# Attention value products of a two-layer hybrid mixer: issued in groups of two key tiles and two heads

## The chip, the cores and the metric

The kernel runs on one core of a Trainium2 chip. The metric is the device time of one execution in microseconds (us). It is written in a tile language with a scheduler: the Python code records operations in an order, a scheduler at build time moves them within each engine's list by priority and by its own idea of when their inputs are ready, and the chip then runs each engine's list strictly in that order, with semaphores between the engines. Engines are named as in the profile: PE (TensorE matmul), PEld (its weight load), DVE (VectorE), ACT (ScalarE), POOL (GpSimd) and SP (the queue that issues the transfers).

## The reference

Two layers of a mixer run over 640 tokens: 512 latent tokens and 128 context tokens. Each layer projects the modulated input with one matrix, runs three head groups on it, projects back and applies a layer norm. The two attention groups matter here:

```python
def gqa_attention(q, k, v):            # 8 query heads, 2 key/value heads, head width 64
    s = einsum('bqgrd,bkgd->bgrqk', qb, k) * scale
    p = softmax(s, axis=-1)
    return einsum('bgrqk,bkgd->bqgrd', p, v)

def diff_attention(q, k, v, lam):      # 4 heads, two softmax maps each, width 32 per map
    s = einsum('bqhmd,bkhmd->bhmqk', qb, k) * scale
    p = softmax(s, axis=-1)
    a = p[:, :, 0] - lam * p[:, :, 1]
    return einsum('bhqk,bkhd->bqhd', a, v)
```

Latent queries read 640 keys: 128 cached context keys and 512 latent ones. That is five key tiles of 128. Everything is float32.

## The kernel before, in words

All 640 tokens go through together. A layer has a main phase and an output phase. In the main phase a background stream (`bg_stream`) computes the input projection in 14 chunks of 256 columns. Weights and activations are split into a high part rounded to the matmul type fp32r and a low part, and each product is made of three matmuls (L347 to L349 with the weights as the stationary operand on the output of tokens by columns, L368 to L370 the other way). The weight chunks come by transfer (`wraw`, L237); ACT casts the high part `wh` (L257) and DVE subtracts to get the low part `wl` (L258).

Around this background, foreground streams are recorded step by step by a small planner (`drive`), which charges each step a planned PE time and a latency from the table `COST`. One stream scores queries against keys and finds the row maximum and sum (`s_pass`: PE L990 and L994 into the one bank pair `pS`, DVE maximum L997, ACT exponential L998). Another (`pv_stream`) makes the attention output. For two heads at a time, `pv_steps` goes over the five key tiles `kt`. `st_tile` makes the transposed score tile of keys by 512 queries in a bank `pB` (L1049 for the differential heads, L1046 and L1047 for the grouped ones; `bankB` has three buffers), and ACT takes its exponential into a tile `PT` (L1055). One step later the value product (L1111, called PV below) multiplies `PT` by the value tile and adds into the bank `pO`: head `e` writes partitions 64e to 64e+63, so the two heads use two halves of the array's columns. PV is a full float32 matmul, which the trace shows as two records, each 128 rows by 64 columns by 512. There are 16 such passes over key tiles in all (8 per layer), so 160 PV matmuls, 320 records.

`PT` tiles come from a pool of 49 general buffers. `mm` is the matmul call, `act` the activation call, `tc.high_priority()` tells the scheduler to put what is recorded inside ahead of other ready work.

Of the kernel before, what the change touches and what calls it, by code (L numbers as in the profile page):

```python
# [11 lines left out]
AF = mybir.ActivationFunctionType  # L12
# [62 lines left out]
def hybrid_kernel(ctx: ExitStack, tc: tile.TileContext, A, cst, outs):  # L75
# [10 lines left out]
    def gran(shape=(128, T), dt=F32, name="g"):  # L86
        t = gp.tile(list(shape), dt, tag="g", name=name)
        return t
# [23 lines left out]
    def bankB():  # L112
        return bank("B")
# [10 lines left out]
    mm = nc.tensor.matmul  # L124
    act = nc.scalar.activation
    dve = nc.vector
    tt = nc.vector.tensor_tensor
    stt = nc.vector.scalar_tensor_tensor

    def barrier():  # L130
        es = ExitStack()
        for e in (nc.scalar.engine, nc.vector.engine, nc.tensor.engine):
            es.enter_context(tc.issue_after(next(i for i in reversed(nc.cur_bb.bb.instructions) if i.engine == e)))
        return es
# [905 lines left out]
    def st_mm(ps, it, kt, two):  # L1040
        qs = slice(0, 512) if kt < 5 else slice(512, 640)
        q1, q2 = it["q1"][:, qs], it["q2"][:, qs]
        k1, k2 = (it[k][:, 128 * kt:128 * kt + 128] for k in ("k1", "k2"))
        n = 4 if kt < 5 else 8
        if two:
            mm(out=ps, lhsT=k1, rhs=q1, start=True, stop=False)  # L1046
            mm(out=ps, lhsT=k2[0:64 + n], rhs=q2[0:64 + n], start=False, stop=True)  # L1047
        else:
            mm(out=ps, lhsT=k1[0:96 + n], rhs=q1[0:96 + n], start=True, stop=True)  # L1049

    def st_tile(it, kt, two):
        ps = bankB()
        st_mm(ps, it, kt, two)
        pt = gran((128, 512), name="PT")
        act(pt, ps, AF.Exp)  # L1055
        return pt

    def st_ctx(items, two):
        ps = bankB()
# [46 lines left out]
    def pv_steps(items, two, value, o):  # L1106
        ready = []
        for kt in range(6):
            now = [st_tile(items[e], kt, two) for e in range(2)] if kt < 5 else []
            for e, pt in enumerate(ready):  # L1110
                mm(out=o[64 * e:64 * e + 64], lhsT=value(kt - 1, e), rhs=pt, start=kt == 1, stop=kt == 5)  # L1111
            ready = now
            yield cost["pv_e" if kt == 5 else "pv_g" if two else "pv_d"]

    def diff_pv(l, m, items, nlam, of):
        dv, cv = items[0]["v"]
        o = bankO()

        def value(kt, e):
            rows = slice(64 * e, 64 * e + 64)  # L1120
            return cv[:, rows] if kt == 0 else tok(dv)[:, kt - 1, rows]

        yield from pv_steps(items, False, value, o)
        if m == 0:
            nc.scalar.copy(of[:, 0:512], o)
        else:
            stt(out=of[:, 0:512], in0=o, scalar=nlam, in1=of[:, 0:512], op0=ALU.mult, op1=ALU.add)
# [76 lines left out]
    def gqa_pv(g, items, mf):  # L1204
        av, avc = items[0]["v"]
        o = bankO()
        cols = slice(64 * g, 64 * g + 64)
        yield from pv_steps(items, True, lambda kt, e: avc[:, cols] if kt == 0 else tok(av)[:, kt - 1, cols], o)
        nc.scalar.copy(mf[:, 0:512], o)
# [63 lines left out]
    with in_order(nc.scalar.engine, nc.vector.engine, nc.tensor.engine):  # L1273
        for j in range(4):
# [5 lines left out]
            ps = bankB()  # L1280
            for k in range(KB):
                q = k % 4
                mm(out=ps[32 * q:32 * q + 32], lhsT=sc[:, k, :], rhs=rw[k].rearrange("p s c -> p (s c)"),
                   start=(k < 4), stop=(k >= 4))
# [16 lines left out]
            for i in range(2):  # L1301
                k = 2 * j + i
# [11 lines left out]
    with barrier():  # L1314
# [4 lines left out]
        first = [gran(name="tk"), gran(name="tk")]  # L1319
# [3 lines left out]
        for l in range(L):  # L1323
            *h, defer = layer(l, h, first, defer)
            first = None
# [70 lines left out]
```

## Time and profile before

| | |
|---|---|
| median of 3 runs | 986.04 us (984.52 to 993.87) |
| the profiled execution's own time | 984.84 us |
| its span in the trace | 983.1 us |
| PE busy | 932.2 us (95%) |
| DVE busy | 599.0 us (61%) |
| ACT busy | 586.8 us (60%) |
| mean granted TensorE clock | 0.988 of full speed |

A record of a matmul on PE lasts until its result is written, and the next one starts before that. What a matmul costs the engine is therefore read as the distance from its start to the next start, not as its duration. Rows of a timeline merge neighbours of one kind; the count behind the x is of records.

### The profile page before, as it was taken

Reading aid. Unit: us, or ns where it says so; the run is one execution under the profiler, and the core shown is the slowest. Engines: PE = TensorE matmul, PEld = TensorE weight load, DVE = VectorE, ACT = ScalarE, POOL = GpSimd, SP = SyncE. Lnnn points to the kernel's source line nnn. Section 1 sums busy time; section 2 is a strip of 40 time slices with the busy share of each in tenths; the row PEclk is TensorE's granted clock in tenths of the full one; section 3 lists DMA queues with packets and bytes.
Section 4 is the critical chain, followed back from the end, with each engine's and each line's share of the span. In section 5 each row is a group of like instructions: output and inputs, shape, how many; then the busy total and the mean of one; then the engine's idle time right before and its main releaser. Section 6 shows DMA issues by size and latency. Waiting matters only on the chain.

```text
span 983.1 us, 20532 instructions
## 1 busy us (share of the span) xinstructions
PE 932.2 (95%) x8197; PEld 745.4 (76%) x8197; DVE 599.0 (61%) x1325; ACT 586.8 (60%) x1313; POOL 98.6 (10%) x132
## 2 busy tenths in 40 slices
PE   6999899999999989999998999999999998999995
PEld 3698676886677748786987997778677765777895
DVE  3356457755767754443799355794596875544467
ACT  2335766566665748874265357755876776787322
POOL 1000002000000001110046000020000101011014
PEclk8999999999999989999999999999999999999998
DMA  9855520443431030225523463024124121202332
GB/s 292 289 157 149 157 66 27 129 137 102 121 91 51 23 97 23 70 83 180 177 80 105 140 152 87 24 59 120 53 78 113 30 79 41 70 23 80 122 111 97
DMA packets 103584, 100.37 MB, mean 102 GB/s; under 512 B 9416, under 2 KB 91840, under 8 KB 103488
## 3 DMA queue, kind: packets, MB, share of 16 engines
q1 hardware_dynamic: 103488, 99.05, 34.1%
q8 instruction: 65, 1.06, 0.5%
q14 instruction: 31, 0.25, 0.1%
HBM read 77.25 MB, written 6.31 MB: 85 GB/s over the span
## 4 chain that ended last, share of the span: by engine, by line
PE 74%; DVE 12%; ACT 7%; DMA 3%; issue 2%; SPq 0%; POOL 0%; DVEq 0%; ACTq 0%
PE pO L1111 10%; PE pA L347 8%; PE pA L349 8%; PE pA L348 8%; PE pA L368 5%; PE pA L369 5%; PE pA L370 5%; PE pS L990 5%; PE pB L1049 2%; PE pB L1046 2%; PE pB L1047 2%; PE pS L994 2%; DMA wraw<-in_w_in_dram 2%; PE pB L276 2%; PE pA L1257 1%
## 5 line engine op out<-in xcount | busy, mean ns | idle before, releaser
L997 DVE TENSOR_REDUCE nmx<-pS 128x1 f32<-128x640 f32 x128 | 105.3, 823 | 133.3 <-PE pS L990 74.9
L347 PE MATMUL pA<-wh,mh 128*128 128x256 f32 x600 | 172.1, 287 | 0.9 <-DVE gate_t L383 0.9
L349 PE MATMUL pA<-wh,ml 128*128 128x256 f32 x600 | 170.1, 284 | 0.2 <-POOL ml L336 0.2
L348 PE MATMUL pA<-wl,mh 128*128 128x256 f32 x600 | 170.0, 284 | 0.0
L257 ACT CAST wh<-wraw 128x512 fp32r<-128x512 f32 x144 | 86.1, 618 | 81.2 <-PE pA L349 31.9
L258 DVE TENSOR_TENSOR wl<-wraw,wh 128x512 fp32r<-128x512 f32 x144 | 97.5, 700 | 56.9 <-ACT wh L257 56.4
L998 ACT ACTIVATE pS<-pS,nmx 128x640 f32<-128x640 f32 x128 | 98.2, 767 | 51.2 <-DVE nmx L997 49.3
L347 PEld LDWEIGHTS pA<-wh,mh 128*128 128x128 f32 x600 | 114.7, 191 | 8.3 <-issue 5.4
L349 PEld LDWEIGHTS pA<-wh,ml 128*128 128x128 f32 x600 | 114.6, 191 | 2.3 <-issue 1.6
L348 PEld LDWEIGHTS pA<-wl,mh 128*128 128x128 f32 x600 | 114.7, 191 | 1.2 <-issue 1.0
L1055 ACT ACTIVATE PT<-pB 128x512 f32<-128x512 f32 x160 | 90.1, 597 | 21.6 <-PE pB L1047 10.6
L1111 PE MATMUL pO<-PT,tk 128*64 128x512 f32 x256 | 89.5, 615 | 1.5 <-ACT PT L1055 1.4
L347 PE MATMUL pA<-wh,hh 128*128 128x256 f32 x240 | 70.2, 293 | 1.3 <-DVE gate_t L383 1.3
L368 PE MATMUL pA<-hh,wh 128*128 128x320 f32 x224 | 71.4, 319 | 0.0
L368 PE MATMUL pA<-mh,wh 128*128 128x320 f32 x224 | 70.9, 317 | 0.0
L369 PE MATMUL pA<-hl,wh 128*128 128x320 f32 x224 | 69.8, 311 | 0.0
L370 PE MATMUL pA<-mh,wl 128*128 128x320 f32 x224 | 69.7, 311 | 0.0
L370 PE MATMUL pA<-hh,wl 128*128 128x320 f32 x224 | 69.6, 311 | 0.0
L369 PE MATMUL pA<-ml,wh 128*128 128x320 f32 x224 | 69.5, 310 | 0.0
L348 PE MATMUL pA<-wl,hh 128*128 128x256 f32 x240 | 69.1, 288 | 0.0
L349 PE MATMUL pA<-wh,hl 128*128 128x256 f32 x240 | 68.8, 287 | 0.0
L347 PEld LDWEIGHTS pA<-wh,hh 128*128 128x128 f32 x240 | 46.2, 192 | 7.6 <-issue 5.3
(285 smaller groups left out, 1960.1 us busy)
## 6 DMA issues: line engine op xcount, KB each, us to landing
wraw<-in_w_in_dram SPq DMA_DIRECT2D x32, 512.0 KB
wraw<-in_w_ada_dram SPq DMA_DIRECT2D x32, 512.0 KB
wraw<-in_w_in_dram SPq DMA_DIRECT2D x48, 256.0 KB
wa<-in_w_ada_dram SPq DMA_DIRECT2D x32, 256.0 KB
wraw<-in_w_out_dram SPq DMA_DIRECT2D x16, 512.0 KB
Q<-Q SPq DMA_DIRECT2D x32, 160.0 KB
KD<-dkh SPq DMA_DIRECT2D x32, 96.0 KB
QD<-dqh SPq DMA_DIRECT2D x32, 80.0 KB
```

Source lines behind the costliest of these rows:

```text
L257: nc.scalar.copy(hi[n], src)
L258: tt(out=lo[n], in0=src, in1=hi[n].bitcast(F32), op=ALU.subtract)
L347: mm(out=ps[:, o:o + 256], lhsT=hi[k][:, sl], rhs=a, start=(n == 0), stop=False)
L348: mm(out=ps[:, o:o + 256], lhsT=hi[k][:, sl], rhs=b, start=False, stop=False)
L349: mm(out=ps[:, o:o + 256], lhsT=lo[k][:, sl], rhs=a, start=False, stop=(n == last))
L368: mm(out=ps, lhsT=wa, rhs=hi[k][:, sl], start=(k == 0), stop=False)
L369: mm(out=ps, lhsT=wa, rhs=lo[k][:, sl], start=False, stop=False)
L370: mm(out=ps, lhsT=wb, rhs=hi[k][:, sl], start=False, stop=(k == KB - 1))
L997: dve.tensor_reduce(out=nmx[:, t, i:i + 1], in_=sv, axis=AX.XY, op=ALU.max, negate=True)
L998: act(sv, sv, AF.Exp, bias=nmx[:, t, i:i + 1], accum_out=den[:, t, i:i + 1])
L1055: act(pt, ps, AF.Exp)
L1111: mm(out=o[64 * e:64 * e + 64], lhsT=value(kt - 1, e), rhs=pt, start=kt == 1, stop=kt == 5)
```

## The change

`st_tile` hands back, with the tile, the instruction of its exponential. `pv_steps` collects tiles until four are there (key tiles 0 and 1 of both heads, then 2 and 3), and issues their four PV matmuls in one high-priority block, in the order tile, then head. The first of the four gets a semaphore dependency on the exponential of the last of the four. The two products of key tile 4 follow as a group of two. The scores, exponentials, values and sums are the same. The title given to the change also names the low parts of the weights on VectorE; L258 already does that, and the diff has no line on it. From the second hunk on, the lines of the changed kernel stand 4 to 10 lines lower (PV L1111 is L1117, L1049 is L1053, L1046 and L1047 are L1050 and L1051, L1055 is L1059, L990 is L994, L994 is L998, L347 to L349 are L351 to L353).

```diff
+    def after(ins, first):
+        tc.add_manual_dep(ins, first.name, mybir.DependencyInfo(
+            mybir.DependencyClass.Sync, mybir.DependencyReason.DATA), reason="after")
...
         pt = gran((128, 512), name="PT")
-        act(pt, ps, AF.Exp)
-        return pt
+        return pt, act(pt, ps, AF.Exp).ins
...
             now = [st_tile(items[e], kt, two) for e in range(2)] if kt < 5 else []
-            for e, pt in enumerate(ready):
-                mm(out=o[64 * e:64 * e + 64], lhsT=value(kt - 1, e), rhs=pt, start=kt == 1, stop=kt == 5)
-            ready = now
+            if len(ready) == 4 or kt == 5:
+                with tc.high_priority():
+                    for i, (pt, _) in enumerate(ready):
+                        k = kt - len(ready) // 2 + i // 2
+                        x = mm(out=o[64 * (i % 2):64 * (i % 2) + 64], lhsT=value(k, i % 2), rhs=pt, start=k == 0,
+                               stop=k == 4)
+                        if i == 0:
+                            after(x.ins, ready[-1][1])
+                ready = []
+            ready += now
             yield cost["pv_e" if kt == 5 else "pv_g" if two else "pv_d"]
```

The scheduler places all of PE's list anew. Over the whole list, the 160 PV matmuls stand before in 96 unbroken runs: 43 of one matmul, 47 of two, 1 of three and 5 of four. They stand now in 43 runs: 11 of two, 27 of four and 5 of six. DVE, ACT, POOL and SP hold the same instructions as before; no instruction of DVE or ACT moves by more than 12 places in its list, POOL's list is the same, and SP exchanges some neighbouring transfers.

The first place is PE in the first layer, at the first pass over key tiles of the differential heads. Before (QD and KD are queries and keys, dcv the cached values, tk the latent ones):

```order
L1049 MATMUL pB<-QD,KD 128x512
L348 MATMUL pA<-wl,hh 128x256
L349 MATMUL pA<-wh,hl 128x256
L1049 MATMUL pB<-QD,KD 128x512 x2
L347 MATMUL pA<-wh,hh 128x256
L1049 MATMUL pB<-QD,KD 128x512
L1111 MATMUL pO<-PT,dcv 64x512
L990 MATMUL pS<-KD,QD 128x320 x2
L1111 MATMUL pO<-PT,dcv 64x512
L348 MATMUL pA<-wl,hh 128x256
```

And now:

```order
L1053 MATMUL pB<-QD,KD 128x512
L352 MATMUL pA<-wl,hh 128x256
L353 MATMUL pA<-wh,hl 128x256
L351 MATMUL pA<-wh,hh 128x256
L352 MATMUL pA<-wl,hh 128x256
L353 MATMUL pA<-wh,hl 128x256
L994 MATMUL pS<-KD,QD 128x320 x2
L351 MATMUL pA<-wh,hh 128x256
L352 MATMUL pA<-wl,hh 128x256
L1117 MATMUL pO<-PT,dcv 64x512 x2
L1117 MATMUL pO<-PT,tk 64x512 x2
L353 MATMUL pA<-wh,hl 128x256
```

The two heads of key tile 0, which stood apart with a score product between them, stand side by side, and both heads of key tile 1 follow at once. Projection matmuls fill the place between the last score product that the group needs and the group.

The second place is PE at the end of the second layer's main phase, in the last pass over key tiles, where hardly any projection work is left. Before:

```order
L1111 MATMUL pO<-PT,tk 64x512
L1034 MATMUL pB<-identr,mhc 8x128
L1046 MATMUL pB<-Q_10233,k_8675 128x512
L1047 MATMUL pB<-Q_10213,k_8676 128x512
L1046 MATMUL pB<-Q_10214,k_8675 128x512
L1047 MATMUL pB<-Q_10234,k_8676 128x512
L1111 MATMUL pO<-PT,tk 64x512
L349 MATMUL pA<-wh,ml 128x256
L347 MATMUL pA<-wh,mh 128x256
```

And now:

```order
L1117 MATMUL pO<-PT,avc 64x512 x2
L1117 MATMUL pO<-PT,tk 64x512 x2
L1050 MATMUL pB<-Q_10214,k_8675 128x512
L1051 MATMUL pB<-Q_10234,k_8676 128x512
L1050 MATMUL pB<-Q_10233,k_8675 128x512
L1051 MATMUL pB<-Q_10213,k_8676 128x512
L1050 MATMUL pB<-Q_10214,k_8675 128x512
L1051 MATMUL pB<-Q_10234,k_8676 128x512
L1050 MATMUL pB<-Q_10233,k_8675 128x512
L1051 MATMUL pB<-Q_10213,k_8676 128x512
L1050 MATMUL pB<-Q_10214,k_8675 128x512
L1051 MATMUL pB<-Q_10234,k_8676 128x512
```

The score products of three key tiles now follow each other with no PV between them; behind the last row shown stand six PV matmuls in one run.

## Rows read from the trace of the kernel before

**Rows 1.** The page: busy time by engine, and the chain by engine and line.

```profile
PE 932.2 (95%) x8197; PEld 745.4 (76%) x8197; DVE 599.0 (61%) x1325; ACT 586.8 (60%) x1313; POOL 98.6 (10%) x132
...
PE 74%; DVE 12%; ACT 7%; DMA 3%; issue 2%; SPq 0%; POOL 0%; DVEq 0%; ACTq 0%
PE pO L1111 10%; PE pA L347 8%; PE pA L349 8%; PE pA L348 8%; PE pA L368 5%; PE pA L369 5%; PE pA L370 5%; PE pS L990 5%; PE pB L1049 2%; PE pB L1046 2%; PE pB L1047 2%; PE pS L994 2%; DMA wraw<-in_w_in_dram 2%; PE pB L276 2%; PE pA L1257 1%
```

**Rows 2.** Busy time in the two main phases: from:to us, length, then engines.

```profile
95.00:463.00 368.00, 353.33 (x3236) 265.10 (x3235) 218.06 (x460) 243.01 (x545) 26.33 (x36) 0.99 0.31 91
...
590.00:917.00 327.00, 318.23 (x2971) 242.99 (x2969) 204.94 (x422) 231.24 (x518) 25.60 (x36) 1.00 0.25 72
```

**Rows 3.** PE's timeline, a split pair: start, us, instruction, records.

```profile
118.42 1.07 PE L1111 MATMUL pO<-PT,dcv 128*64 128x512 f32 x2
119.42 0.56 PE L990 MATMUL pS<-KD,QD 96*128 96x320 f32 x2
119.91 1.07 PE L1111 MATMUL pO<-PT,dcv 128*64 128x512 f32 x2
120.92 0.39 PE L348 MATMUL pA<-wl,hh 128*128 128x256 f32 x1
```

**Rows 4.** PE's timeline, two heads side by side.

```profile
133.12 0.28 PE L348 MATMUL pA<-wl,hh 128*128 128x256 f32 x1
133.25 0.28 PE L349 MATMUL pA<-wh,hl 128*128 128x256 f32 x1
133.46 1.08 PE L1111 MATMUL pO<-PT,tk 128*64 128x512 f32 x4
134.47 0.38 PE L347 MATMUL pA<-wh,hh 128*128 128x256 f32 x1
134.69 0.28 PE L348 MATMUL pA<-wl,hh 128*128 128x256 f32 x1
134.81 0.28 PE L349 MATMUL pA<-wh,hl 128*128 128x256 f32 x1
```

**Rows 5.** PE's timeline, four PV matmuls in one run.

```profile
365.92 1.94 PE L1111 MATMUL pO<-PT,tk 128*64 128x512 f32 x8
367.79 1.12 PE L538 MATMUL pB<-sq,cs 128*128 128x512 f32 x2
```

**Rows 6.** The instructions of L1111: weight load, ns min/median/max.

```profile
L1111 PEld LDWEIGHTS pO<-PT,tk x256: 132/136/137, 122.5 to 913.8; 128*64 128x64 f32 x128
```

**Rows 7.** Timeline of PE and ACT: a score product and its exponential.

```profile
448.85 0.40 PE L1047 MATMUL pB<-Q,k 68*128 68x512 f32 x1
...
449.29 0.60 ACT L1055 ACTIVATE PT<-pB 128x512 f32<-128x512 f32 x1 [1.44 <-PE pB L1047]
```

**Rows 8.** Timeline of PE and ACT: exponentials and PVs that waited for them.

```profile
153.22 0.62 ACT L1055 ACTIVATE PT<-pB 128x512 f32<-128x512 f32 x1
153.31 1.65 PE L1111 MATMUL pO<-PT,dcv 128*64 128x512 f32 x4 [0.26 <-ACT PT L1055]
154.90 0.38 PE L349 MATMUL pA<-wh,hl 128*128 128x256 f32 x1
...
905.48 0.62 ACT L1055 ACTIVATE PT<-pB 128x512 f32<-128x512 f32 x1
906.15 1.07 PE L1111 MATMUL pO<-PT,tk 128*64 128x512 f32 x2 [1.04 <-ACT PT L1055]
```

**Rows 9.** Who waited for the exponential L1055: us, times.

```profile
PEld pO L1111: 6.2, 17
...
PE pO L1111: 1.7, 3
```

**Rows 10.** ACT and DVE by line: busy us, mean ns, idle before.

```profile
L998 ACT ACTIVATE pS<-pS,nmx 128x640 f32<-128x640 f32 x128 | 98.2, 767 | 51.2 <-DVE nmx L997 49.3
L257 ACT CAST wh<-wraw 128x512 fp32r<-128x512 f32 x144 | 86.1, 618 | 81.2 <-PE pA L349 31.9
L258 DVE TENSOR_TENSOR wl<-wraw,wh 128x512 fp32r<-128x512 f32 x144 | 97.5, 700 | 56.9 <-ACT wh L257 56.4
L997 DVE TENSOR_REDUCE nmx<-pS 128x1 f32<-128x640 f32 x128 | 105.3, 823 | 133.3 <-PE pS L990 74.9
```

## The prediction, made before the changed kernel ran

> **What bounds the kernel now.** I read the page first. PE is busy for 932.2 of 983.1 us, DVE and ACT for about 60%, and PE holds 74% of the chain that ended last, of which PV (L1111) is the longest single line with 10% [rows 1]. The two main phases hold every PV. There PE is busy for 353.3 of 368 us and for 318.2 of 327 us, while ACT reaches 66% and 71% and DVE 59% and 63% [rows 2]. The lines by engine say the same from the other side: DVE sat idle for 133.3 us before its maximum L997, mostly for PE's score product, and ACT for 81.2 us before its weight cast, mostly for PE to free a buffer [rows 10]. So in these phases PE is the engine that everybody waits for, and a microsecond less of PE's own work there should come out of the time, unless something else is close behind.
>
> Next I read what one PV costs, as the distance from start to next start in PE's timeline. A PV with one head alone takes from 118.42 to 119.42, 1.00 us; its partner, after a score product, from 119.91 to 120.92, 1.01 us more [rows 3]. Two heads side by side take from 133.46 to 134.47, **1.01 us for both** [rows 4]: they write different column halves and run at the same time. Four in a run take 365.92 to 367.79, 1.87 us [rows 5], so each further pair in a run costs 0.86 us. A run has a price at its ends too. The projection matmul before it is followed after 0.21 us (133.25 to 133.46) and the one behind it after 0.22 us (134.47 to 134.69), where such matmuls follow each other after 0.12 us (134.69 to 134.81) [rows 4]. That is 0.09 going in and 0.10 coming out, 0.19 us per run.
>
> **The change, part by part.** (1) *Pairs that were split become whole, and pairs join.* Before there are 43 runs of one, 47 of two, 1 of three and 5 of four. At 1.00, 1.01, 1.87 (a pair and a single, taken as two pairs) and 1.87 us [rows 3 to 5] they make 43.0 + 47.5 + 1.9 + 9.4 = 101.8 us. This fits the chain, where L1111 holds 10% of 983.1 us [rows 1]. Now there are 11 runs of two, 27 of four and 5 of six: 11 x 1.01 + 27 x 1.87 + 5 x (1.87 + 0.86) = 11.1 + 50.5 + 13.7 = 75.3 us. The term is **-26.5 us**. About 22 us of it come from the 43 singles, which are 21 to 22 pairs paid twice; the rest from joining pairs.
>
> In a run of four the second pair's weight loads are hidden: 1.87 us for four is 0.15 us less than twice 1.01 us [rows 4, 5], and the new runs are of that kind, so I take that row. The Trainium skill, "TensorE: Matmul & The Clock Gate", Part 3 on packing small matmuls, says that a weight load overlaps running matmuls only when its row group differs; all PV weights use all 128 rows, so by that rule the second pair's loads would be exposed. By the row the term stays at -26.5 us, by the rule it would shrink to about -10 us (a rival below); the trace does not agree with the rule here.
>
> (2) *Fewer ends of runs.* 96 runs become 43: 53 x 0.19 = **-10.1 us** [rows 4]. The lower bound is about 5 us, because some removed ends lay beside other full float32 work rather than beside projection matmuls.
>
> (3) *The added wait.* The first PV of a group now waits for the last of four exponentials, and PE runs in order, so projection, scores and everything else of PE queue behind it; DVE's maximum and ACT's exponential of the score stream follow late in turn. What the wait needs: from a score product's start to its exponential 0.44 us (448.85 to 449.29) [rows 7], from there to the PV that waited for it 0.67 us (905.48 to 906.15) [rows 8], together 1.11 us with ACT free, and up to 1.5 us when the other head's exponential of 0.60 us is just ahead. I add up, by the spacings above, the PE work that stands in the new order between the last score product needed and each of the 43 groups: 24 groups have 1.5 us or more, 19 have less, and of these five have less than 1.1 us. The missing parts sum to 1.5 us (need 1.1) to 6 us (need 1.5). Below, the term can be a gain: before, a pair could start with one head and stall inside for the other, as at 153.31, where it took 1.59 us instead of 1.01 [rows 8], and all waits for exponentials at PV come to 1.7 us on PE and 6.2 us on its weight loads [rows 9]. Above, every group could wait the 1.04 us that is the longest such wait shown [rows 8]: 45 us. I take **+5 us**, near the low end, because most groups have cover. It includes the end of the second layer's phase, where ten score matmuls now stand in a row with only three banks and six exponentials of 0.60 us behind them; that is a wait of one or two us.
>
> (4) *What PE does not pass on.* In the two phases PE already idles for 23.5 of 695 us [rows 2]. With less work in front of it, some of its gain will be spent waiting for ACT, DVE or a transfer. ACT would go from 243 of 368 to 243 of about 349 us, 70%, so it does not become the bound. I take a tenth, **+3.7 us**; the ends are nothing and half (18 us).
>
> (5) *Costed at nothing.* The same exponentials and score products run. Two more `PT` tiles are alive at a time, of 49 buffers; had they made the pool short, transfers and casts would have had to move, and the lists of DVE and ACT hardly move. Exchanged transfers on SP lie beside PE work; cover gone, a late weight chunk costs a few us. The low parts of the weights are on VectorE in 144 instructions before [rows 10] and after, so that half of the change's name is worth 0.
>
> **Sum.** -26.5 - 10.1 + 5 + 3.7 = -28 us against the profiled execution's 984.84 us gives **957 us**. The median of the runs, 986.04 us, lies 1.2 us above that execution, which I leave inside the range.
>
> **The rivals.**
> - *Half is given back.* Denser groups hold PE for 1.87 or 2.73 us at a time, during which the score stream gets nothing; its loop through one bank pair (DVE 823 ns, ACT 767 ns) then starts late and PE later lacks work. For it: the loop has 128 rounds and one buffer. Against: DVE waits for PE in that loop, not the other way [rows 10]. Price: 18 us instead of 3.7, 971 us. Chance 0.14.
> - *Weight loads exposed.* There are 27 + 2 x 5 = 37 further pairs in the new runs and 5 to 6 in the old, so 31 more. If the two loads of each head, 136 ns each [rows 6], were not hidden, a further pair would cost 4 x 0.136 = 0.54 us more: 17 us, 974 us. The run of four in the trace, 1.87 us [rows 5], speaks against it. The Trainium skill's page "TensorE: Matmul & The Clock Gate" would have it so. Chance 0.03.
> - *The rest of PE's list got worse by as much.* The scheduler placed everything anew; a late score tile or weight chunk here and there could eat the gain. Result 976 to 995 us, about 985. Against: the other engines' lists are nearly the same. Chance 0.09.
> - *Slower: the group waits in ACT's queue.* The place is PE in front of each group. If one score exponential (767 ns) and one weight cast (618 ns) stand before the needed exponential on ACT [rows 10], a group waits 1.4 us beyond its cover; over 43 groups that is 60 us, and 984.8 - 36.6 + 60 = 1008 us. It decides from a mean wait of 36.6 / 43 = 0.85 us; slower by over 1% from 1.08 us. For it: ACT is at 66% and the block is put forward as early as the scheduler believes possible. Against: 24 of the 43 groups have cover of 1.5 us or more, so the other 19 would have to wait about 2 us each on average. Chance 0.06.
>
> **How the numbers follow.** The forecast, 942 to 967 us, has 0.68. Its low end is the full 36.6 us plus the 6.2 us of old waits on weight loads gone, 942; its high end has the wait at 10 us and a quarter lost. With the rival of half the gain (0.14) the range is 942 to 977 us. One per cent, about 10 us, is what a measurement can tell from no change: faster by more than that has 0.68 + 0.14 + 0.03 = 0.85, within it 0.09, slower 0.06.
>
> **What would show it.** In the changed trace, step 1: no PV run of two records; runs of eight records 1.87 us to the next start, the line L1117 about 8% of the chain. Step 2: 43 runs with 0.2 us at each end. Step 3: PE and its weight loads waiting at L1117 for L1059 for about 5 us more than the 7.9 us now; 45 us would mean the last rival. Step 4: PE's idle time in the two phases, now 23.5 us, grown by single microseconds; by 15 or more, the first rival. Runs of eight records over 2.3 us would mean exposed loads. The prediction is wrong if PE's work falls as summed and the time does not follow.

## The result, and the profile after

The changed kernel takes **972.87 us** (median of 4 runs, 971.27 to 973.73) against 986.85 us for the kernel before in the same session (4 runs): ratio 0.9854, 95% interval 0.9825 to 0.9884. It is faster by 14 us. The forecast was 957 us with a gain of 28 us, so half of the forecast gain came, and the time lies 6 us above the range of 942 to 967 us. The medians below leave out one execution of e5, which took 1025.07 us at a granted clock of 0.831.

The page of the changed kernel, profiled in an execution of 972.11 us with a span of 970.3 us: busy time by engine, then the chain by engine and by line.

```profile
PE 909.5 (94%) x8197; PEld 751.7 (77%) x8197; DVE 600.3 (62%) x1325; ACT 585.4 (60%) x1313; POOL 99.5 (10%) x132
...
PE 65%; DVE 13%; ACT 9%; DMA 9%; issue 3%; SPq 1%; POOL 0%; DVEq 0%; ACTq 0%; POOLq 0%
PE pA L351 8%; PE pA L353 8%; PE pA L352 8%; PE pO L1117 8%; PE pA L372 4%; PE pS L994 4%; PE pA L374 4%; PE pA L373 4%; DMA wraw<-in_w_in_dram 3%; DMA wa<-in_w_ada_dram 2%; PE pB L1053 2%; PE pS L998 2%; PE pB L1050 2%; PE pB L1051 2%; ACT
```

PE's busy time fell by 22.7 us, from 932.2 [rows 1] to 909.5. The span fell by 12.8 us, from 983.1 to 970.3. So PE's idle time in the span rose from 50.9 to 60.8 us. PE's share of the chain fell from 74% [rows 1] to 65%, and DVE, ACT and DMA took what it lost: the path now goes through other engines more often. Later weight chunks are not behind it: ACT's casts waited 25.6 us for the input projection's transfers before and wait 20.2 us now.

The two main phases of the changed kernel, in the columns of [rows 2] (from:to, length, busy time of PE, PEld, DVE, ACT and POOL, granted clock, share and GB/s of the DMA engines); each begins and ends with about the same work as there.

```profile
95.00:450.00 355.00, 336.42 (x3218) 266.06 (x3217) 218.12 (x459) 241.01 (x544) 27.02 (x36) 0.98 0.32 92
578.00:904.50 326.50, 311.57 (x2988) 247.34 (x2986) 206.96 (x423) 232.72 (x521) 25.85 (x36) 0.98 0.25 72
```

PE idles for 18.6 + 14.9 = 33.5 us of them, 10.0 us more than before, and the granted clock is 0.98 in both where it was 0.99 and 1.00 [rows 2]. The first phase shrank by 13 us, the second by half a microsecond.

The PV runs themselves, in PE's timeline of the changed kernel:

```profile
121.62 0.57 PE L994 MATMUL pS<-KD,QD 96*128 96x320 f32 x2
122.03 0.28 PE L351 MATMUL pA<-wh,hh 128*128 128x256 f32 x1
122.15 0.28 PE L352 MATMUL pA<-wl,hh 128*128 128x256 f32 x1
122.36 1.08 PE L1117 MATMUL pO<-PT,dcv 128*64 128x512 f32 x4
123.26 1.03 PE L1117 MATMUL pO<-PT,tk 128*64 128x512 f32 x4
124.22 0.39 PE L353 MATMUL pA<-wh,hl 128*128 128x256 f32 x1
124.45 0.46 PE L994 MATMUL pS<-KD,QD 96*128 96x320 f32 x2
124.75 0.63 PE L1053 MATMUL pB<-QD,KD 100*128 100x512 f32 x2
...
162.79 2.79 PE L1117 MATMUL pO<-PT,tk 128*64 128x512 f32 x12
165.51 0.68 PE L875 MATMUL pB<-XQ,XK 64*32 64x32 f32 x56
```

Four products take 122.36 to 124.22, 1.86 us, and six take 162.79 to 165.51, 2.72 us: the spacings of [rows 4, 5]. There are 43 runs and none of one product alone. Summed from each run's start to the next instruction's start, the PVs took 105.3 us before and 76.9 us now; of the 76.9, one run at the lower clock holds 1.8 us too many, so 75.1 us at full clock.

Who PE and its weight loads wait for in the changed kernel (us in total, times, longest):

```profile
PE pB L1038 <- DVE mhc L979: 5.3, 6, 1.6
PE pS L994 <- ACT pS L1002: 4.4, 10, 0.7
...
PE pB L841 <- issue: 3.3, 3, 2.0
...
PE pB L1053 <- ACT PT L1059: 2.3, 1, 2.3
...
PE pB L875 <- DVE XK L865: 2.1, 4, 0.9
...
PE pO L1117 <- ACT PT L1059: 0.9, 2, 0.8
...
PEld pO L1117 <- ACT PT L1059: 6.8, 20, 1.2
...
PEld pB L1038 <- ACT PT L1059: 3.6, 3, 1.8
```

The groups hardly wait: 0.9 us on PE and 6.8 us on its weight loads, where the single products waited 1.7 and 6.2 us [rows 9]. The new idle time stands at other lines, in small pieces. The transposition of the context maxima, L1038, waited 2.3 us in 2 waits before and waits 5.3 us in 6. The two rows for L1053 and L875 stood at 0.4 and 0.2 us before, the one for L841 at 1.6 us.

One such wait, and what follows it, in PE's timeline of the changed kernel:

```profile
719.91 0.31 PE L374 MATMUL pA<-mh,wl 128*128 128x320 f32 x1
722.56 0.79 PE L1053 MATMUL pB<-QD,KD 100*128 100x512 f32 x1 [2.34 <-ACT PT L1059]
723.15 0.31 PE L1038 MATMUL pB<-identr,mhc 128*8 128x128 f32 x1
723.54 0.79 PE L1053 MATMUL pB<-QD,KD 100*128 100x512 f32 x1
724.26 1.98 PE L1117 MATMUL pO<-PT,dcv 128*64 128x512 f32 x4
726.02 1.92 PE L1117 MATMUL pO<-PT,tk 128*64 128x512 f32 x4
727.87 0.80 PE L1053 MATMUL pB<-QD,KD 100*128 100x512 f32 x1
```

ACT's timeline at the same place:

```profile
721.20 0.83 ACT L574 ACTIVATE hs<-hs,lbs 128x640 f32<-128x640 f32 x1 [1.86 <-DVE hs L573]
721.93 2.06 ACT L1059 ACTIVATE PT<-pB 128x512 f32<-128x512 f32 x4
```

And the stretches around it by window, changed kernel:

```profile
713.00:722.50 9.50, 6.92 (x45) 6.11 (x44) 8.71 (x25) 7.50 (x21) 0.00 (x0) 1.00 0.20 58
...
722.50:729.40 6.90, 6.76 (x17) 2.78 (x18) 5.22 (x13) 2.69 (x6) 0.00 (x0) 0.51 0.00 0
729.40:735.00 5.60, 5.60 (x34) 4.17 (x33) 2.29 (x4) 3.94 (x7) 0.00 (x0) 1.00 0.39 94
```

L1053 needs a bank that an exponential has to empty. That exponential stands in ACT's queue behind a gate activation, which waits 1.86 us for DVE, and DVE is busy for 8.71 of these 9.5 us. So PE arrives earlier than before and waits. Right behind the wait the granted clock is 0.51, that is 1.2 GHz, for 6.9 us, and the run of four takes 3.61 us (724.26 to 727.87) in place of 1.86.

The same place in the kernel before, by window:

```profile
723.00:732.50 9.50, 9.11 (x60) 8.13 (x58) 9.28 (x28) 8.09 (x21) 1.06 (x2) 1.00 0.26 73
733.00:741.00 8.00, 8.00 (x35) 3.87 (x35) 5.70 (x16) 3.97 (x10) 0.00 (x0) 1.00 0.46 126
```

There PE was busy for 9.11 of 9.5 us, waited 0.35 us for the same exponential, and the clock stayed at 1.00. DVE had 9.28 us of work in it. PE had been a little slower than DVE here; now it is ahead of DVE, and being ahead earns nothing.

The changed kernel's PE has nine stretches at 1.2 GHz, 36 us in all (at 19, 108, 153, 296, 347, 511, 723, 808 and 965 us); before it had four, 23 us (at 18, 301, 353 and 977 us). If PE worked through all of them, half of the 13 us more is lost, 6.5 us. It is the same number that the mean clocks give: 983.1 x (1 - 0.988) = 11.8 us lost before and 970.3 x (1 - 0.981) = 18.4 us lost after, **6.6 us** more. Taking that out of the busy time leaves PE's work at full clock: 932.2 - 11.8 = 920.4 us before, 909.5 - 18.4 = 891.1 us after. The span's change is then, by construction, the sum of three terms:

**-29.3 us of work, +6.6 us of clock, +9.9 us of idle time = -12.8 us.**

The split is good to a few us. PE is busy in only 13.9 us of the slow stretches before and in 30.3 us now; half of that is 8.2 us more of lost clock, and the work would then have fallen by 30.9 us.

### The profile page after: what moved, and what is told of

It reads as the page before. It is cut to its first block, busy times and chain, and to the rows that moved or that the text cites. A ratio compares the mean times of both kernels' runs of the same rounds, so it can differ in the third digit from the quotient of the medians.

```text
span 970.3 us, 20533 instructions
## 1 busy us (share of the span) xinstructions
PE 909.5 (94%) x8197; PEld 751.7 (77%) x8197; DVE 600.3 (62%) x1325; ACT 585.4 (60%) x1313; POOL 99.5 (10%) x132
## 4 chain that ended last, share of the span: by engine, by line
PE 65%; DVE 13%; ACT 9%; DMA 9%; issue 3%; SPq 1%; POOL 0%; DVEq 0%; ACTq 0%; POOLq 0%
PE pA L351 8%; PE pA L353 8%; PE pA L352 8%; PE pO L1117 8%; PE pA L372 4%; PE pS L994 4%; PE pA L374 4%; PE pA L373 4%; DMA wraw<-in_w_in_dram 3%; DMA wa<-in_w_ada_dram 2%; PE pB L1053 2%; PE pS L998 2%; PE pB L1050 2%; PE pB L1051 2%; ACT pS L1002 2%
## 5 line engine op out<-in xcount | busy, mean ns | idle before, releaser
L1001 DVE TENSOR_REDUCE nmx<-pS 128x1 f32<-128x640 f32 x128 | 105.3, 823 | 117.9 <-PE pS L994 68.2
L351 PE MATMUL pA<-wh,mh 128*128 128x256 f32 x600 | 171.9, 287 | 1.6 <-DVE gate_t L387 1.3
L353 PE MATMUL pA<-wh,ml 128*128 128x256 f32 x600 | 171.0, 285 | 0.4 <-POOL ml L340 0.2
L351 PEld LDWEIGHTS pA<-wh,mh 128*128 128x128 f32 x600 | 115.2, 192 | 4.5 <-DVE gate_t L387 2.0
L353 PEld LDWEIGHTS pA<-wh,ml 128*128 128x128 f32 x600 | 115.1, 192 | 2.1 <-issue 0.7
L1059 ACT ACTIVATE PT<-pB 128x512 f32<-128x512 f32 x160 | 89.2, 598 | 27.5 <-PE pB L1053 16.0
L351 PE MATMUL pA<-wh,hh 128*128 128x256 f32 x240 | 70.8, 295 | 1.3 <-DVE gate_t L387 1.3
L353 PE MATMUL pA<-wh,hl 128*128 128x256 f32 x240 | 70.1, 292 | 0.0
L1117 PE MATMUL pO<-PT,tk 128*64 128x512 f32 x256 | 64.5, 610 | 0.2 <-ACT PT L1059 0.2
L351 PEld LDWEIGHTS pA<-wh,hh 128*128 128x128 f32 x240 | 47.4, 198 | 4.0 <-DVE gate_t L387 2.1
```

The costliest lines, as they stand in the source:

```text
L351: mm(out=ps[:, o:o + 256], lhsT=hi[k][:, sl], rhs=a, start=(n == 0), stop=False)
L353: mm(out=ps[:, o:o + 256], lhsT=lo[k][:, sl], rhs=a, start=False, stop=(n == last))
L1001: dve.tensor_reduce(out=nmx[:, t, i:i + 1], in_=sv, axis=AX.XY, op=ALU.max, negate=True)
L1059: return pt, act(pt, ps, AF.Exp).ins
L1117: x = mm(out=o[64 * (i % 2):64 * (i % 2) + 64], lhsT=value(k, i % 2), rhs=pt, start=k == 0, stop=k == 4)
```

## The experiments

The question was where over half of the removed PE work went. The same three terms are read from the page and the granted clock of each profiled run; "lost" is span x (1 - clock), work is busy time without it. Medians are of a kernel's runs; a profiled execution may lie some us beside them.

| kernel | median, us | PE work | lost to 1.2 GHz | idle | span |
|---|---|---|---|---|---|
| before | 986.9 | 920.4 | 11.8 | 50.9 | 983.1 |
| changed | 972.9 | 891.1 | 18.4 | 60.8 | 970.3 |
| e1_pairs | 975.3 | 894.2 | 22.4 | 59.1 | 975.7 |
| e3_late | 977.3 | 882.8 | 28.3 | 65.8 | 976.9 |
| e4_half | 960.9 | 861.8 | 24.9 | 70.8 | 957.5 |
| e9_held_pairs | 975.6 | 895.9 | 22.4 | 54.5 | 972.8 |
| e10_held_fours | 988.5 | 890.2 | 28.7 | 70.8 | 989.7 |
| e11_held_fill | 973.0 | 890.3 | 24.4 | 61.5 | 976.2 |
| e12_b_max | 983.0 | 915.4 | 15.7 | 47.9 | 979.0 |
| e13_a_max | 969.4 | 883.4 | 21.2 | 57.7 | 962.3 |
| e14_more | 1002.4 | 918.4 | 18.0 | 63.7 | 1000.1 |

The work column is not exact. e12 keeps PE's list of the kernel before and e13 that of the changed kernel, and it still falls by 5.0 and 7.7 us in them. A matmul's record lasts longer than the distance to the next start (0.28 against 0.12 us for a projection matmul above), so a wait shorter than the difference counts as busy. Differences of this size in the column show little.

### Groups of two, no added wait, groups one step later

Three variations of the changed kernel's block. Groups of two instead of four:

```diff
-            if len(ready) == 4 or kt == 5:
+            if len(ready) == 2 or kt == 5:
```

> One part of the change: groups of two (one key tile, both heads) instead of four, still forward and still waiting for the last exponential. PV runs: 66 of two, 7 of four, so 66 x 1.01 + 7 x 1.87 = 79.8 us against 101.8 before, and 23 fewer run ends (4.4 us): 26 us less PE work. Theory P (other waits take back over half of any PE work saved, here and in the change alike): about 976 us, PE's shown waits up by some 5 us. Theory G (it is the wait for four exponentials and the blocks of 1.87 us that took the gain back): about 962 us, faster than the change's 972.9 us.

975.3 us, ratio 0.9881 (0.986 to 0.9902): theory P's number. The runs are 66 of two and 7 of four, so the singles are what counts; the change, which joins the pairs as well, is 2.4 us faster, and the two intervals overlap. The products wait more here, though: 22.9 us on PE and its weight loads against 7.7 in the changed kernel, so this run does not take the wait for the exponentials away.

The change without the dependency on the group's last exponential:

```diff
-                        if i == 0:
-                            after(x.ins, ready[-1][1])
```

> The change without the dependency on the last of the four exponentials. The scheduler then breaks the groups: 100 runs, 46 of one, 48 of two, 6 of three, so the PV work is about 106 us as before. Theory that the gain of the change comes from joined runs: about 986 us, no change from before. Theory that the forward place of the products brings the gain: about 973 us, as the change.

1015.1 us, ratio 1.029 (1.0271 to 1.0308), slower than the kernel before and outside both expectations. The scheduler pulled the group apart again (46 runs of one product) and put each product forward as far as it could. Weight loads of this kernel that waited:

```profile
PEld pO L1117 <- ACT PT L1059: 30.7, 85, 1.6
```

85 waits for the exponentials, 30.7 us, against 20 and 6.8 us with the dependency. In the trace they show inside the pairs: the PVs sum to 128.6 us, where they took 105.3 before. The high priority alone costs 28 us; the wait that the prediction priced at +5 us is what keeps the group whole.

Each group of four one step later, to have its exponentials long done:

```diff
-            if len(ready) == 4 or kt == 5:
+            if len(ready) == 6:
+                group = ready[:4] if kt < 5 else ready
...
-                ready = []
+                ready = ready[len(group):]
```

> The change with the group of key tiles 0 and 1 recorded one step later (at key tile 3) and 2, 3 and 4 together at the end: 16 runs of four and 16 of six, 73.6 us of PV work, 32 runs. PE work 28 + 12 = 40 us less than before. Every group's exponentials lie a step back, so that no group but the six should wait. Theory P (over half is taken back wherever it is saved): about 969 us. Theory G (waits in front of the groups took it): about 955 us.

977.3 us, ratio 0.9909 (0.9888 to 0.993). PE's work fell by a further 8 us (16 runs of six), and all of it was lost again to the clock and to waits. P's own number, 969, was too low, and G's, 955, far too low. But the edit did not do what it was made for: the groups wait 11.7 us here (7.9 on weight loads, 3.8 on PE) against 7.7 in the changed kernel. So neither this run nor the one before settles theory G. What speaks against it is the changed kernel itself, whose groups wait no longer than the single products did, 7.7 against 7.9 us.

### Less work in the groups

In the changed kernel the PV products of key tiles 1 to 4 are taken over 256 of the 512 queries; half of these products is left out.

```diff
+                        c = 256 if k else 512
-                        x = mm(out=o[64 * (i % 2):64 * (i % 2) + 64], lhsT=value(k, i % 2), rhs=pt, start=k == 0,
+                        x = mm(out=o[64 * (i % 2):64 * (i % 2) + 64, 0:c], lhsT=value(k, i % 2), rhs=pt[:, 0:c],
```

> The change with the value products of key tiles 1 to 4 on 256 of the 512 queries: the rest of those products is left out. 64 pairs cost 0.43 us less, 27 us of PE work, with no operation elsewhere removed. If PE sets the time as the prediction had it: 972.9 - 25 = 948 us. Theory P (PE's work is worth about 0.4 of itself now): 962 us.

960.9 us, ratio to before 0.9742 (0.9724 to 0.976), 12 us below the changed kernel. Its page:

```profile
PE 886.7 (93%) x8197; PEld 753.1 (79%) x8197; DVE 600.1 (63%) x1325; ACT 583.5 (61%) x1313; POOL 100.0 (10%) x132
```

PE's work fell by 29.3 us, the same amount as in the change itself, and again 10.0 us came back as idle time and 6.5 us as lost clock. (The scheduler redrew the list a little, to 46 runs, and the edit was counted as 27 us; the rest lies within what the column is good for.) So the shortfall is no property of grouping alone: about 29 us less of PE's work is worth 12 to 13 us once more.

### Other orders

The planner that writes the order was given other numbers, in the changed kernel and in the kernel before: its latencies times 1.25 (`lat *= 1.25`), or 0.38 us less for PV on PE.

```diff
+        for k in ("pv_e", "pv_g", "pv_d"):
+            cost[k] = (cost[k][0] - 0.38, cost[k][1])
```

> The change, with every latency that the planner waits out before a stream's next step raised by a quarter, so that more projection work is recorded between a step and the one that needs it. PE's own work stays (runs of two, four, six: 12, 28, 4). Theory L (the order leaves too little work between a step and the one that needs it, now that PE passes through it faster): PE's shown waits fall by some 5 us, about 966 us. Theory S (PE waits wherever an order is laid out that does not fit, and any new order shifts the waits about): within 6 us of 973 us to either side.

> The kernel before with the same raised latencies, nothing of the change: 36 runs of one, 54 of two, 4 of four, some 7 us less PE work than before. Theory L: less than half the gain of the change's variant, about 982 us. Theory S, and theory T (the kernel before has an order whose waits happen to be few, and any redrawing of it adds waits): 987 to 997 us.

> The change with the planner's PE price of each value-product step lowered by 0.38 us, about what joined products save (18 us per layer over 48 steps), so that its clock runs with PE's again. Theory L (the planner's clock now runs ahead of PE): about 965 us. Theory S: 967 to 979 us.

> The kernel before with the same lowered prices: 49 runs of one, 50 of two, 1 of three, 2 of four, PE work within 1 us of before. Theory T (any redrawing of the order of before adds waits): 992 to 1000 us. Theory L: within 4 us of 987 us.

Latencies: changed kernel 988.7 us, ratio 1.0035 (1.0013 to 1.0058), kernel before 1002.1 us, 1.0155 (1.0126 to 1.0185). PV price: 978.1 us, 0.9901 (0.9872 to 0.9929), and 1003.2 us, 1.0172 (1.0155 to 1.0189). Every redrawing cost time: 5 to 16 us. Only the changed kernel with the PV price came out in a range that was given (theory S); the other three are slower than any. Within the same redrawing the change is worth 13.4 and 25.1 us. This left open whether the change had lost its other half to a redrawn order (theory T). So the order was held.

### The order held

From the kernel before, with a table of each engine's order and an ordering edge between neighbours, only PE's list is edited: in the first kernel the earlier product of each split pair moves down to the later one; in the second all products of a group of four or six move down to the last.

```diff
+    for kind, text in HELD.items():
+        mine = [i for i in nc.cur_bb.bb.instructions if i.engine == getattr(mybir.EngineType, kind) ...]
+        ...
+                tc.add_manual_dep(mine[at], last, mybir.DependencyInfo(
+                    mybir.DependencyClass.NoSync, mybir.DependencyReason.DATA), reason="held")
```

> The kernel before with the list of every engine held as the scheduler made it, by orderings without semaphores, except that on PE the first head's value product is moved down to stand beside the second's wherever the two stood apart: 70 runs of two and 5 of four in place of 96 runs. DVE, ACT, POOL and SP keep their lists instruction by instruction. PE work falls by 22 us for 21.5 pairs and 21 x 0.19 = 4 us of run ends, 26 us. Theory T (what the change lost, it lost by the redrawn order of PE): most of it comes out, 964 to 970 us. Theory P (other waits take back over half of any PE work saved): 975 us or more.

975.6 us, ratio 0.9888 (0.9854 to 0.9921). With the lists of all other engines unchanged, 24.5 us of PE work bring 11 us. Theory T falls: the loss doesn't need a redrawn order. Of what is missing in the profiled execution, 10.6 us stand in the clock column and 3.6 in the idle time, so in this kernel the lower clock took more than the waits that show.

> The same, with the products of key tiles 0 and 1, and of 2 and 3, of both heads moved down to stand beside the last of the four: the runs of the change (13 of two, 29 of four, 3 of six) in the old order of everything else. PE work 37 us less. Theory T: 954 to 962 us, well under the change's 972.9 us. Theory P: 970 us or more, as the change.

988.5 us, ratio 1.0022 (1.0003 to 1.0042). PE's work is that of the changed kernel to 1 us, and the time is 15.6 us longer; theory T had 954 to 962 us, and theory P the change's own time. Who PE waits for in this kernel (L1044 is the score product, L1088 the transposition of the context maxima):

```profile
PE pS L1044 <- ACT pS L1052: 11.2, 20, 1.2
PE pB L1088 <- DVE mhc L1029: 9.7, 7, 2.4
```

4.1 and 2.3 us before. These waits fit one reading: the products had stood between an instruction of PE and the next that needs its result through DVE and ACT, and moved down behind that next one, they no longer cover the way through the other engines.

### The waits filled

The changed kernel with its lists held; on PE, projection matmuls from at most 3 us behind are pulled in front of 23 instructions that waited.

> The changed kernel with the lists of all engines held as they are, and on TensorE alone 109 projection matmuls (L351 to L353, L372 to L374) pulled from at most 3 us behind to the front of the 23 instructions before which the changed kernel's profile shows TensorE waiting (17.3 us of waits in all; the 109 matmuls are 14.3 us of work). Nothing is added or left out. Theory W (the freed time sits in single waits, each made by a dependent that stands too early in TensorE's list, and the clock falls follow those waits): the waits shrink by 10 us or more, the granted clock rises from 0.98 towards 0.99, and the time is 957 to 964 us. Theory P (TensorE's list is paced by the other engines' chains; what is filled here waits a few us later): the waits shrink by 4 us at most and the time is 968 to 974 us. If the pulled matmuls themselves wait for their activations or weights, the time is above 975 us and the waits stand at L351 to L374.

973.0 us against the changed kernel's 972.9; ratio to before 0.9841 (0.9811 to 0.9871). PE's waits sum to 49.0 us, as in the changed kernel (49.2), and PE's idle time is 61.5 us. The fill did what it should where it was put: compared instruction by instruction, waits of 11.9 us went away, and waits of 11.9 us came up at other instructions. So theory W falls and P stands: a matmul that fills one wait is missing elsewhere, and the chains through the other engines end no earlier.

### The score steps

The prediction's first rival put the loss on the score steps' loop through VectorE and ScalarE. Both kernels with lists held; the maximum is taken over one half of the score columns (the scores scaled down).

```diff
-                dve.tensor_reduce(out=nmx[:, t, i:i + 1], in_=sv, axis=AX.XY, op=ALU.max, negate=True)
+                dve.tensor_reduce(out=nmx[:, t, i:i + 1], in_=ps[:, 0:1, 0:320], axis=AX.XY, op=ALU.max, negate=True)
```

> The kernel before, the lists of all engines held as they are, with VectorE's score maximum (L997, 823 ns, 128 times) taken over one half of the 640 columns, so some 0.4 us less in each score step and some 50 us less of VectorE's work; the scores are scaled down so that exponentials stay finite. It leaves out half of the maximum. First control for the changed kernel with the same edit. Theory S (the score steps' chain through VectorE and ScalarE is what paces TensorE): 970 to 982 us. Theory D (the pacing is spread over single chains elsewhere and the clock): 982 to 988 us.

> The changed kernel, lists of all engines held, with the same edit (score maximum over half of the columns, scores scaled down; it leaves out half of the maximum). Theory S (the freed time is caught by the score steps): the changed kernel gains more from it than the kernel before, the difference between the two grows from 14 us to 20 to 28 us, the time is 945 to 960 us. Theory D (the freed time is caught by single chains elsewhere, such as the context sums, and by the clock): the difference stays at 10 to 17 us and the time is 965 to 973 us.

The edit does shorten the loop. The maximum in the changed kernel, where it took 823 ns:

```profile
L1056 DVE TENSOR_REDUCE nmx<-pS 128x1 f32<-128x320 f32 x128 | 62.8, 490 | 132.5 <-PE pS L1049 76.8 <-PE pS L1053 55.0
```

The kernel before goes to 983.0 us, ratio 0.9947 (0.9926 to 0.9968), the changed kernel to 969.4 us, 0.9799 (0.9764 to 0.9834). 128 steps shorter by a third of a microsecond bring 4 to 5 us to either, and the difference between the two stays at 13.6 us; the idle time differs by 9.8 us, as before. Theory S falls, and with it the mechanism of that rival, as far as VectorE's part of the loop goes; ScalarE's part was not shortened. The wait shown above stays, at 2.17 us, as no score maximum stands in front of it.

### More work in the groups

Lists held, the changed kernel issues the first key tile's products three times inside the first group of each head pair:

```diff
-                    for i, (pt, _) in enumerate(ready):
+                    for i, (pt, _) in enumerate(ready[:2] * (2 if kt == 2 else 0) + ready, -4 if kt == 2 else 0):
```

> The changed kernel, lists of all engines held, with the products of the first key tile issued three times (the first two results are overwritten), inside the first group of each of the 16 head pairs: 32 further pairs in runs that exist already, at 0.86 us each from the runs of four, so 27.5 us more of TensorE's own work; nothing else moves. Theory P (this list passes on under half of what TensorE's work changes by, in either direction, since other chains carry the rest): 982 to 988 us. Theory K (the kernel before stood at a corner: work that is added is on the path in full, and only work that is removed meets the other chains): 996 to 1002 us; then waits shrink little.

1002.4 us, ratio to before 1.017 (1.0136 to 1.0205), 29.5 us above the changed kernel. Its page:

```profile
PE 936.4 (94%) x8325; PEld 757.6 (76%) x8325; DVE 599.8 (60%) x1325; ACT 585.1 (59%) x1313; POOL 100.3 (10%) x132
```

27.3 us of work are added, and neither the idle time (+2.9 us) nor the lost clock (-0.4 us) gives any of it back. Theory K holds: added work is on the path in full, while removed work counted at under half (in e4 12 of 29.3 us, in the profiled executions of the change 12.8 of 29.3, in e9 11 of 24.5). This kernel has the work of the kernel before to 2 us and takes 15.6 us longer. So it isn't the sum of PE's work that decides but where it stands. That the products of the kernel before lay between waits and covered them is the reading that fits; no run here moves them back one by one.

No version that does all of the work beats the changed kernel.

## Where the prediction held and where it failed

By its own last sign the prediction is wrong: PE's work fell by four fifths of what was summed, and the time by less than half.

**What bounds the kernel.** Right in part of the first layer, incomplete in the second. The score maximum's starts show it, being the same DVE instruction in both kernels. Before, then after:

```profile
574.82 0.82 DVE L997 TENSOR_REDUCE nmx<-pS 128x1 f32<-128x640 f32 x1 [2.70 <-PE pS L990]
```

```profile
564.19 0.82 DVE L1001 TENSOR_REDUCE nmx<-pS 128x1 f32<-128x640 f32 x1 [2.70 <-PE pS L994]
```

This is the 65th of 128. The changed kernel leads by 1.4 us at the 32nd, by 9.3 us at the 48th, by 10.6 us here, by 9.2 us at the 96th and by 12.3 us at the 128th. Most of the gain came between the 32nd and the 48th (252.9 to 340.9 us before), where 15 of the 43 singles stood; the second layer has 16 of them and brought about two us more. PE's 95% busy was read as a sign that everybody waits for PE. But busy times of 59 and 63% on DVE [rows 2] are averages over stretches; in some of them (the 9.5 us shown above) DVE was as full as PE.

**(1) PV runs, -26.5 us.** Right: 105.3 to 75.1 us at full clock is -30.2 us, 43 runs, no single product, 1.86 us for four and 2.72 for six. The 75.3 us summed for now is met; the 105.3 us before are 101.8 us of products, as summed, and 3.6 us of waits inside the runs, which are gone. The weight loads stay hidden in every new run at full clock. The Trainium skill, "TensorE: Matmul & The Clock Gate", Part 3, has one sentence that lets them overlap only where the row group differs; all use the same 128 rows here, and the trace disagrees by its 1.86 us for four. The rival of exposed loads falls.

**(2) Fewer ends of runs, -10.1 us.** The price was right; the sum did not show. An end costs what was read beside a projection matmul (122.15 to 122.36 is 0.21 us, 124.22 to 124.45 is 0.23 us) and beside a score product too: the one between two single PVs took 0.49 us from start to start [rows 3], the one at 124.45, with no PV beside it, takes 0.30 us. That is 0.19 us for one end out and one in. But PE's work fell by 29.3 us, and the PVs alone make up 30.2 of it, so in busy time nothing is left for the removed ends; short waits that count as busy took their place. An estimate from the spacings avoids that: each is held against the usual one of the same matmul between the same neighbours in the traces here, at full clock. By it PE's undisturbed work fell by 26.6 us in the PVs and by 3 to 7 us in all the rest, where 10.1 were summed.

**(3) The added wait, +5 us.** Too high, on the safe side: PE's and its weight loads' waits at the groups are 7.7 us against 7.9 before. The exponentials came in time, so the cover that was counted was enough.

**(4) What PE does not pass on, +3.7 us.** This is the step that failed. Measured are 9.9 us of idle time and 6.6 us of lost clock, 16.5 of 29.3 us. By the estimate from the spacings, which counts the short waits too, waiting grew by 12 to 15 us and the lost clock by 6. PE's idle time in the two phases grew by 10.0 us, between the single microseconds that were expected and the 15 us that were to show the first rival. A tenth was taken, since PE idled little and ACT at 70% would not become the bound; no row gave the tenth itself. Those shares say how much an engine waited, not how close the next wait was behind it. The bound of a half was named and kept for the range only. With (3) too high by 5 us, the idle time alone, 9.9 us against 8.7 in both terms, would have come out almost right, by luck.

**The clock** was not in the sum at all. It stood in the trace: 0.99 and 1.00 in the two phases [rows 2] left no room above and much below. That a longer wait of PE may be followed by 1.2 GHz was not asked. The Trainium skill, "TensorE: Matmul & The Clock Gate", Part 1, says that the throttled state is the default and that activity releases it; the 0.51 behind the wait of 2.34 us agrees. What the clock costs by itself was not tried apart from the waits. Among runs of one and the same kernel it shows: over 161 runs of 16 kernels, 0.01 of mean clock goes with 6.7 us (standard error 0.4). The changed kernel's mean over its 4 runs is 0.9795, that of the kernel before 0.9857 over 74 runs: by this about 4 us of the difference between the medians.

**The sum.** -36.6 became -29.3 in busy time (7.3 us short, most of it short waits), waits 9.9 in place of 8.7 (1.2 short), clock 6.6 in place of nothing: together the 15 us between -28 and -12.8.

**The rivals.** "Half is given back" has the right number, 971 us, and that is luck: its mechanism is wrong, since shortening the score loop left the difference as it was. "The rest of PE's list got worse" is partly what happened, but e9 shows it with all other lists unchanged. The slow rival, groups waiting in ACT's queue, needed 0.85 us for each group and got 0.18 (7.7 us over 43), no more than before; e2 shows how it would have looked.

**What stays open.** Which chain ends each of the new waits is known for the places shown, not for all of them, and that DVE was as full as PE is shown for one stretch alone. Why the clock falls behind some waits and not behind others is open: at 108 us both kernels wait 1.31 us for `gate_t` after the same instructions, and only the changed kernel's clock falls, to 0.51.

## What to carry to other kernels

Before removing work from the engine that is 95% busy, look at the stretches, not the phases: where a second engine is as full in the same ten microseconds, less work there may earn nothing, as at the place shown. Ask of each product that is moved what it stood between: in an in-order list, work that lies between a result's departure and its return is cover, and taking it away can be worth less than adding it costs (0.4 against 1.0 here). Read a saving from the distances between starts and not from busy time alone, in which short waits hide, and price TensorE's waits twice, once as waiting and once as the slower clock that may follow.

## What the runs showed of the hardware that was not expected

- The mean granted clock of one program on one core differs from run to run, and its time with it: one and the same kernel (e11) took 965.76 us at 0.988 and 977.98 us at 0.975. A comparison to 1% needs the clock of each run beside it.
- Runs of four, six and (in e14) eight PV products keep 0.86 us for each further pair at full clock, with the four weight loads of 0.13 us between them hidden throughout.
- The same PE work, to 2 us in the table, took 986.9 us (before) and 1002.4 us (e14), and 972.9 us (changed) and 988.5 us (e10): where the work stands counted for as much as the change.
